# HGRN scores in eight steps with the next pair's preparation between them, and the sums of h taken from kept transposes, one a slot

## The chip, the cores and the metric

The kernel runs on one core of a Trainium2 chip. The metric is the device time of one execution in microseconds. The core has a matrix engine (TensorE, PE in the profile, with its weight loads as PEld), VectorE (DVE), ScalarE (ACT), GpSimd (POOL) and SyncE (SP), which issues DMAs. Each engine works through its own instructions in order; where one needs another's result, it waits on a semaphore.

## The reference

One block of an encoder over 256 positions of width 2048, all in float32:

```
u   = rms_norm(x)                 # over 2048
z   = u @ w_in                    # hq hf hi hg (1024 each), aq ak av (1024 each), gates (4096)
y_a = HGRN2 recurrence of 8 heads on hq hf hi, norm per head, times silu(hg)
y_b = chunked attention of 16 heads on aq ak av, relative bias
h   = x + (sig(gate_a) * (y_a @ w_branch_a) + sig(gate_b) * (y_b @ w_branch_b)) @ w_out
out = rms_norm(h + relu(rms_norm(h) @ w_up)**2 @ w_down)      # w_up 2048x8192, w_down 8192x2048
```

The recurrence is S_t = diag(g_t) S_(t-1) + k_t v_t^T, o_t = S_t^T q_t with g = lb + (1 - lb) * sigmoid(f), k = 1 - g, q = silu(z) / sqrt(128). Written as scores, position t attends to s <= t with q_t * k_s * exp(b_t - b_s), where b is the running sum of log g (started anew every 64 positions, with the decays of whole chunks multiplied in).

## The kernel before, in words

**Products.** Every weight is split into a high part `wh` (ScalarE's cast, line 89) and a remainder `wl` (VectorE's subtraction, line 90), each piece 128x1024, and a product is made of three matmuls, high x high, high x low, low x high (lines 143 to 145 for row blocks, 184 to 188 for transposed ones). So each 128x1024 piece of weights costs a DMA on SP, a cast and a subtraction, and both stand in the queues of ScalarE and VectorE among all else that these do. The casts and subtractions are given priority over the code around them, so the scheduler may set them ahead of it.

**The HGRN stage.** The heads come in pairs, four pairs u = 0 to 3. `fq(u)` makes f and z of a pair (for pairs 2 and 3 by two products, hf and hq) and prepares them: `hf_pair` (lines 310 to 326) scales f, takes the sigmoid, makes kk = 1 - f and clamps f (lines 319, 320), takes the logarithm on ScalarE and the running sum b by a scan on VectorE (line 324); `hq_pair` (lines 328 to 339) makes q from z (line 335) with two copies of odd columns times f (line 338).

`hgrn_scores` makes a pair's scores at several distances. The diagonal (line 372) multiplies kk by q on PE; VectorE writes it into `sd` by a product with the identity (line 373) and a predicated copy (line 374). For each level B = 2, 8, 32, `factors` makes exp(b_end - b) (`el`, lines 383, 384), exp(b - b_start) (`er`, 388, 389 or 393 to 397) and the ratios `rr` (390, 391), the differences on VectorE, the exponentials on ScalarE, and from them `kl` (399) and `qr` (403 to 405); `level` multiplies them on PE (line 416) and copies the result into `sd` under masks (line 423). `factors128` and `level128` (line 448) do the same across the two halves of 128 positions. The five steps of a pair are: diagonal and factors 2; level 2 and factors 8; level 8 and factors 32; level 32 and factors128; level128.

`hgrn_out` makes outputs from scores and values: per head pair and half, `po` on PE (lines 476, 477), its squares on ScalarE (481), their sum (482), `ms` (95), the power on GpSimd (96) and `o` (487), the last two times two; `finish` transposes o (494) and splits it.

These steps are spread by hand over the matmuls of other products: `later` puts steps in the list `behind`, each with a number, `tick` is called once or twice for each 128 rows of a weight, and when a step's number has been counted down it is issued there. All `ps` and `po` tiles share two PSUM buffers (tag `sm`). The order before: pairs 0 and 1 are both prepared at once, then pair 0's scores with a first gap of 20 and gaps of 8, queued ahead of hi (values, `v_chunk(0)`), pair 1's with gaps of 8, then hg, then hf and hq of pair 2, then `group(0)` queues the outputs of the first two pairs, pair 2's scores with gaps of 6, hf and hq of pair 3, values, pair 3's scores, hg, `group(1)`, and the first two products of the attention stage.

**The units.** From the gates on, 512x512 blocks of products go by a scheme of seven block products instead of eight, `Unit` and `run` (lines 725 to 915). It needs sums of blocks of the left matrix: `combos` (lines 632 to 660) adds each block's high and low part into a fresh token buffer (line 640), subtracts and adds these in place (651, 655 to 657) and splits the four results, `S5`, `S4`, `S2`, `S7`. Where `blocks` is given, it takes those instead of line 640's sums; the units of the MLP do so. A unit has some eleven slots, at which `step` issues one entry of its list of steps, if the slot's number is at least the entry's third member, or else the unit's `start`. `plain` issues at once all leading entries whose first member is at most the quarter of the left matrix that it needs.

Unit `wo0` and unit `wo2` make h = x + m @ w_out in four column blocks. During `wo2`, the steps `h_blocks(0)` transpose the blocks 0 and 1 of h (`tp_h`, line 106, two PSUM buffers), scale them by the norm's weights (`hw`, line 981), split them into `act_h`, take the sums of squares on ScalarE (line 983), and make the four sums `S_h` for the next unit, `up00`. In `up00`, `h_blocks(2)` do the same for blocks 2 and 3, and `factor` makes the norm's factors.

Of the kernel before, what the change touches and what calls it, by code (L numbers as in the profile page):

```python
# [18 lines left out]
NM = T // P  # L19
# [31 lines left out]
def tile_hybrid_block(  # L51
# [6 lines left out]
    x, out = x[0], out[0]  # L58
# [100 lines left out]
    def later(*steps):  # L159
        behind.extend([n, f] for n, f in steps)  # L160
# [45 lines left out]
    steps = [1, 1] + [2] * (KD // 2 - 1)  # L206
# [103 lines left out]
    def hf_pair(u, f):  # L310

        nc.vector.tensor_tensor(f, f, bc(rstd_t, 1, 2), op=ALU.mult)
        nc.scalar.activation(f, f, AF.Sigmoid)
        for h in range(2):
            hh = 2 * u + h
            nc.vector.tensor_scalar(f[:, h, :], f[:, h, :], omlb[:, hh:hh + 1], lb[:, hh:hh + 1],
                                    op0=ALU.mult, op1=ALU.add)
        kk = h2(f"kk{u}")
        nc.vector.tensor_scalar(kk, f, -1.0, 1.0, op0=ALU.mult, op1=ALU.add)
        nc.vector.tensor_scalar(f, f, LN_MIN, None, op0=ALU.max)  # L320
        lg = h2(f"lg{u}")
        nc.scalar.activation(lg, f, AF.Ln)
        b = h2(f"b{u}")
        nc.vector.tensor_tensor_scan(b.rearrange("p h t -> p (h t)"), reset,
                                     lg.rearrange("p h t -> p (h t)"), 0.0, ALU.mult, ALU.add)
        return f, kk, b

    def hq_pair(u, z, g):

        nc.vector.tensor_tensor(z, z, bc(rstd_t, 1, 2), op=ALU.mult)  # L330
        s = h2(f"sq{u}")
        nc.scalar.activation(s, z, AF.Sigmoid)
        q = hp.tile([P, 2, NM, 192], F32, name=f"q{u}", tag="q", bufs=2)
        half = lambda a: a.rearrange("p h (m t) -> p h m t", t=P)
        nc.vector.scalar_tensor_tensor(q[:, :, :, 0:P], half(z), DK ** -0.5, half(s), op0=ALU.mult, op1=ALU.mult)
        odd = lambda a: a.rearrange("p h m (j u) -> p h m j u", u=2)[:, :, :, :, 1]
        for h in range(2):
            nc.vector.tensor_tensor(q[:, h, :, P:], odd(q[:, :, :, 0:P])[:, h], odd(half(g))[:, h], op=ALU.mult)
        return q

    def v_chunk(g):
        acc = gemm(xT, w_in_n, C_HI + g * NC, KD, f"hi{g}")
        vs = []
        for m in range(NM):
            v = hp.tile([P, NC], F32, name=f"v{g}{m}", tag="tok", bufs=7)
            nc.scalar.activation(v, acc[:, m, :], AF.Copy, scale=rstd[:, m:m + 1])
            vs.append(v)
        return vs

    def hg_chunk(g):  # L350
        acc = gemm(xT, w_in_n, C_HG + g * NC, KD, f"hg{g}")
        gws = []
        for m in range(NM):
            s = hp.tile([P, NC], F32, name=f"gw{g}{m}", tag="tok", bufs=7)
            nc.scalar.activation(s, acc[:, m, :], AF.Sigmoid, scale=rstd[:, m:m + 1])
            nc.vector.scalar_tensor_tensor(s, acc[:, m, :], rstd[:, m:m + 1], s, op0=ALU.mult, op1=ALU.mult)
            s3 = s.rearrange("p (h d) -> p h d", d=DK)
            nc.vector.tensor_tensor(s3, s3, bc(hgw, 1, NH), op=ALU.mult)
            gws.append(s)
        return gws  # L360

    def hgrn_scores(n, kk, b, q):

        sd = hp.tile([P, 2, NM, P], F32, name=f"sd{n}", tag="sd", bufs=2)
        so = hp.tile([P, 2, P], F32, name=f"so{n}", tag="so", bufs=2)
        held = {}
# [85 lines left out]
        f = [lambda i=i, B=B: factors(i, B) for i, B in enumerate(LEVELS)]  # L452
        l = [lambda i=i, B=B: level(i, B) for i, B in enumerate(LEVELS)]

        def both(*fs):
            def go():
                for x in fs:
                    x()
            return go

        return (sd, so), [both(diagonal, f[0]), both(l[0], f[1]), both(l[1], f[2]), both(l[2], factors128), level128]

    ya = []

    def hgrn_out(g, h0, sc, vs, gws):
        sd, so = sc
        n = f"{g}{h0}"
        hi, lo = ya[g][:, :, 0, :], ya[g][:, :, 1, :]
        os = []

        def outputs(m):
            po = ps_sm.tile([P, 2, DK], F32, name=f"po{n}{m}", tag="sm")
            for h in range(2):
                c = slice((h0 + h) * DK, (h0 + h + 1) * DK)
                if m:
                    nc.tensor.matmul(po[:, h, :], so[:, h, :], vs[0][:, c], start=True, stop=False)
                nc.tensor.matmul(po[:, h, :], sd[:, h, m, :], vs[m][:, c], start=m == 0, stop=True)
            o = hp.tile([P, 2, DK], F32, name=f"o{n}{m}", tag="o", bufs=4)
            sq = hp.tile([P, 2, DK], F32, name=f"osq{n}{m}", tag="osq", bufs=1)
            s2 = small.tile([P, 2], F32, name=f"os{n}{m}", tag="os")  # L480
            nc.scalar.activation(sq, po, AF.Square)
            nc.vector.tensor_reduce(s2, sq, axis=AX.X, op=ALU.add)
            ro = small.tile([P, 2], F32, name=f"ro{n}{m}", tag="ro")
            rsqrt(ro, s2, DK, 2)
            for h in range(2):
                c = slice((h0 + h) * DK, (h0 + h + 1) * DK)
                nc.vector.scalar_tensor_tensor(o[:, h, :], po[:, h, :], ro[:, h:h + 1], gws[m][:, c],
                                               op0=ALU.mult, op1=ALU.mult)
            os.append(o)

        def finish(m):
            tp = ps_tp.tile([P, 2, P], F32, name=f"tpo{n}{m}", tag="tp")
            for h in range(2):
                nc.tensor.transpose(tp[:, h, :], os[m][:, h, :], ident)
            split(hi[:, h0:h0 + 2, m * P:(m + 1) * P], lo[:, h0:h0 + 2, m * P:(m + 1) * P], tp)

        return [lambda m=m: outputs(m) for m in range(NM)], [lambda m=m: finish(m) for m in range(NM)]

    def fq(u):
        if u == 0:  # L500
            f, z = f0, z0
        elif u == 1:
            f, z = f1, z1
        else:
            f, z = h2(f"f{u}"), h2(f"zq{u}")
            add_parts(f, gemm_t(xT, w_in_t, C_HF + u * T, KD, f"hf{u}"))
            add_parts(z, gemm_t(xT, w_in_t, C_HQ + u * T, KD, f"hq{u}"))
        g, kk, b = hf_pair(u, f)
        return kk, b, hq_pair(u, z, g)


    def scores(n, a, gap, first=None):
        sc, steps = hgrn_scores(n, *a)
        later(*[(gap if i or first is None else first, f) for i, f in enumerate(steps)])
        return sc

    def group(g, s0, s1, vs, gws, gap, gap2):
        o0, f0 = hgrn_out(g, 0, s0, vs, gws)
        o1, f1 = hgrn_out(g, 2, s1, vs, gws)
        later(*[(gap, f) for f in o0 + o1], *[(gap2, f) for f in f0 + f1])  # L520

    ya += [new_act(f"ya{g}") for g in range(2)]
    a0, a1 = fq(0), fq(1)
    s0 = scores(0, a0, 8, 20)
    vs0 = v_chunk(0)
    s1 = scores(1, a1, 8)
    gws0 = hg_chunk(0)
    a2 = fq(2)
    group(0, s0, s1, vs0, gws0, 3, 4)
    s2 = scores(2, a2, 6)  # L530
    a3 = fq(3)
    vs1 = v_chunk(1)
    s3 = scores(3, a3, 6)
    gws1 = hg_chunk(1)
    group(1, s2, s3, vs1, gws1, 2, 3)
    acc_q = [gemm_t(xT, w_in_t, C_AQ + i * T, KD, f"aq0{i}") for i in range(2)]
# [90 lines left out]
    def fours(t):  # L627
        return t.rearrange("p (k t) -> p k t", t=P)
# [340 lines left out]
    hT = []  # L969
    Sh = {}  # L970

    def h_blocks(n0):

        def one(n, m):
            if not m:
                hT.append(new_act(f"h{n}"))
            hi, lo = hT[n][:, :, 0, :], hT[n][:, :, 1, :]
            t = h1[n][m]
            tp = transpose4(t, f"h{n}{m}")
            tmp = fours(token(f"hw_{n}_{m}"))  # L980
            nc.vector.tensor_tensor(tmp, tp, bc(wmlp[:, 4 * n:4 * n + 4], 2, P), op=ALU.mult)
            split(hi[:, :, m * P:(m + 1) * P], lo[:, :, m * P:(m + 1) * P], tmp)
            nc.scalar.activation(token(f"hsq_{n}_{m}"), t, AF.Square, accum_out=ssq2[:, m, n:n + 1])

        def factor():
            ssum2 = small.tile([P, NM], F32, name="ssum2", tag="ssum")
            nc.vector.tensor_reduce(ssum2, ssq2, axis=AX.X, op=ALU.add)
            rsqrt(rstd2, ssum2, D, NM)

        return [(n, lambda n=n, m=m: one(n, m)) for n in (n0, n0 + 1) for m in range(NM)] + [  # L990
            (n0 + 1, f, 7) for f in ([factor] if n0 else combos(hT, "h", sp, Sh))]

    rstd2 = const.tile([P, NM], F32, name="rstd2")

    def h_out(m, n, acc):
        t = token(f"h1_{n}_{m}")
        with tc.high_priority(offset=2000):
# [7 lines left out]
    rstd3 = const.tile([P, NM], F32, name="rstd3")  # L1005
    NQ = 4
    units = [Unit(lambda: mT, lambda: Sm, w_out, n0 * NC, f"wo{n0}", lambda m, n, acc, n0=n0: h_out(m, n0 + n, acc),
                  steps=(lambda: h_blocks(0)) if n0 else (lambda: turned(mT, 3, "m3", ga)), start=3 if n0 else 0) for n0 in (0, 2)]
    fin = {}
    for qd in range(NQ):  # L1010
        last = qd == NQ - 1
# [115 lines left out]
```

## Time and profile before

| | us |
|---|---|
| median of three runs | 1410.29 (1409.94 to 1411.42) |
| the profiled execution | 1411.28 |
| its span in the profile | 1409.5 |
| PE busy (98% of the span) | 1387.3 |
| DVE busy (79%) | 1119.1 |
| ACT busy (64%) | 909.0 |
| POOL busy (10%) | 137.0 |

The granted clock of PE averages 0.997 over the span. The HGRN stage lies between about 10 and 240 us of the profile, the units `wo0` and `wo2` between about 640 and 734, and `up00` follows. A row of instructions has start, duration, engine, line, operation, output <- input, shape and count, and in brackets how long the engine stood idle before it and what released it. `wl_hi` is the remainder of a piece of the weights hi, `act_h` the split transposes of h, `acc_up00c` a PSUM bank of unit up00.

### The profile page before, as it was taken

The numbers are of one execution on the slowest core, as the hardware profiler recorded it, in microseconds if no ns is written. First come the engines' busy times: TensorE is split into PE (matmuls) and PEld (weight loads), VectorE is DVE, ScalarE is ACT, GpSimd is POOL, SyncE is SP. The second block draws the span as 40 slices with busy tenths as digits, with TensorE's granted clock in tenths as the row PEclk, the third lists the DMA queues.
The fourth block names the chain that finished last, engine by engine and source line by source line (L and its number), as shares of the span: only waits on it lengthen the run. The fifth ranks groups of instructions, "written<-read, shape, count | busy, mean of one in ns | idle before, by whom it ended". The sixth has DMA issues, their size and how long they took to land.

```text
span 1409.5 us, 18582 instructions
## 1 busy us (share of the span) xinstructions
PE 1387.3 (98%) x6562; PEld 1149.8 (82%) x6562; DVE 1119.1 (79%) x1410; ACT 909.0 (64%) x1170; POOL 137.0 (10%) x220
## 2 busy tenths in 40 slices
PE   9999999999999999999999999999999999999997
PEld 7878888878787888888778888888888888888885
DVE  7897987675657875687999878789777897878885
ACT  6755745464556665445767876677666876668764
POOL 2000001010000000001210001100111001110200
PEclk9999999999999999999999999999999999999999
DMA  9644445665568987558898898998899888998883
GB/s 336 219 156 156 144 157 162 191 172 167 177 224 262 259 236 257 188 176 254 245 292 263 242 277 225 288 279 249 258 290 292 249 229 252 286 298 261 259 247 118
DMA packets 122925, 327.42 MB, mean 232 GB/s; under 512 B 10944, under 2 KB 11712, under 8 KB 122448
## 3 DMA queue, kind: packets, MB, share of 16 engines
q1 hardware_dynamic: 103264, 264.80, 54.8%
q0 software_dynamic: 18416, 59.84, 21.4%
q10 hardware_dynamic: 1152, 1.60, 0.3%
q8 instruction: 51, 0.84, 0.2%
q14 instruction: 42, 0.34, 0.1%
HBM read 271.67 MB, written 10.49 MB: 200 GB/s over the span
## 4 chain that ended last, share of the span: by engine, by line
PE 93%; DVE 3%; ACT 2%; issue 1%; DMA 0%; POOL 0%; SPq 0%; POOLq 0%; DVEq 0%; ACTq 0%
PE acc_ak L185 2%; PE acc_hq L185 2%; PE acc_aq L185 2%; PE acc_hf L185 2%; PE ps L416 1%; PE tp_u L106 1%; PE acc_ga L144 1%; PE acc_hg L144 1%; PE acc_hg L145 1%; PE acc_hg L143 1%; PE acc_ga L145 1%; PE acc_bb L143 1%; PE acc_ga L143 1%; PE acc_ba L143 1%; PE acc_av L145 1%; PE acc_ba L145 1%
## 5 line engine op out<-in xcount | busy, mean ns | idle before, releaser
L185 PE MATMUL acc_aq<-act_x,wh_aq 128*128 128x512 f32 x128 | 46.6, 401 | 0.0
L185 PE MATMUL acc_hf<-act_x,wh_hf 128*128 128x512 f32 x128 | 45.9, 396 | 0.0
L185 PE MATMUL acc_hq<-act_x,wh_hq 128*128 128x512 f32 x128 | 45.9, 396 | 0.0
L185 PE MATMUL acc_ak<-act_x,wh_ak 128*128 128x512 f32 x128 | 45.2, 398 | 0.0
L90 DVE TENSOR_TENSOR wl_ga<-raw_ga,wh_ga 128x1024 fp32r<-128x1024 f32 x16 | 19.6, 1225 | 19.6 <-ACT wh_ga L89 19.4
L184 PE MATMUL acc_aq<-act_x,wl_aq 128*128 128x256 f32 x120 | 34.9, 291 | 0.0
L184 PE MATMUL acc_hf<-act_x,wl_hf 128*128 128x256 f32 x120 | 34.4, 287 | 0.0
L184 PE MATMUL acc_hq<-act_x,wl_hq 128*128 128x256 f32 x120 | 34.3, 286 | 0.0
L90 DVE TENSOR_TENSOR wl_av<-raw_av,wh_av 128x1024 fp32r<-128x1024 f32 x16 | 19.6, 1224 | 18.1 <-ACT wh_av L89 18.1
L184 PE MATMUL acc_ak<-act_x,wl_ak 128*128 128x256 f32 x120 | 33.8, 281 | 0.0
L89 ACT CAST wh_hg<-raw_hg 128x1024 fp32r<-128x1024 f32 x16 | 16.8, 1050 | 24.2 <-PE acc_hg L145 13.9
L89 ACT CAST wh_bb<-raw_bb 128x1024 fp32r<-128x1024 f32 x16 | 16.9, 1054 | 23.3 <-PE acc_ba L145 17.7
L90 DVE TENSOR_TENSOR wl_bb<-raw_bb,wh_bb 128x1024 fp32r<-128x1024 f32 x16 | 19.6, 1222 | 14.8 <-ACT wh_bb L89 14.8
L89 ACT CAST wh_av<-raw_av 128x1024 fp32r<-128x1024 f32 x16 | 16.8, 1052 | 22.0 <-PE acc_av L145 12.4
L90 DVE TENSOR_TENSOR wl_aq<-raw_aq,wh_aq 128x1024 fp32r<-128x1024 f32 x16 | 19.6, 1223 | 14.2 <-ACT wh_aq L89 14.1
L89 ACT CAST wh_ba<-raw_ba 128x1024 fp32r<-128x1024 f32 x16 | 16.8, 1053 | 20.7 <-PE acc_bb L145 13.8
L89 ACT CAST wh_aq<-raw_aq 128x1024 fp32r<-128x1024 f32 x16 | 16.8, 1048 | 20.0 <-PE acc_hg L145 9.5
L90 DVE TENSOR_TENSOR wl_ba<-raw_ba,wh_ba 128x1024 fp32r<-128x1024 f32 x16 | 19.6, 1223 | 12.4 <-ACT wh_ba L89 12.4
L185 PEld LDWEIGHTS acc_ak<-act_x,wh_ak 128*128 128x128 f32 x128 | 24.0, 188 | 5.6
L185 PEld LDWEIGHTS acc_aq<-act_x,wh_aq 128*128 128x128 f32 x128 | 24.1, 189 | 5.4 <-issue 0.7
L185 PEld LDWEIGHTS acc_hf<-act_x,wh_hf 128*128 128x128 f32 x128 | 24.1, 188 | 5.3 <-DVE f L193 0.3
L185 PEld LDWEIGHTS acc_hq<-act_x,wh_hq 128*128 128x128 f32 x128 | 24.1, 188 | 5.1
(1808 smaller groups left out, 5250.3 us busy)
## 6 DMA issues: line engine op xcount, KB each, us to landing
raw_hi<-in_w_in_n_dram SPq DMA_DIRECT2D x16, 512.0 KB, 4.2
raw_hg<-in_w_in_n_dram SPq DMA_DIRECT2D x16, 512.0 KB, 3.8
raw_aq<-in_w_in_t_dram SPq DMA_DIRECT2D x16, 512.0 KB, 4.0
raw_ak<-in_w_in_t_dram SPq DMA_DIRECT2D x16, 512.0 KB, 3.9
raw_av<-in_w_in_n_dram SPq DMA_DIRECT2D x16, 512.0 KB, 4.4
raw_ga<-in_w_in_t_dram SPq DMA_DIRECT2D x16, 512.0 KB, 4.2
raw_ba<-in_w_branch_a_dram SPq DMA_DIRECT2D x16, 512.0 KB, 4.4
raw_bb<-in_w_branch_b_dram SPq DMA_DIRECT2D x16, 512.0 KB, 4.5
```

The source lines that it names most:

```text
L89: (copy or nc.scalar.copy)(hi, src)
L90: nc.vector.tensor_tensor(lo, src, hi.bitcast(F32), op=ALU.subtract)
L106: nc.tensor.transpose(tp[:, j, :], src[:, j * P:(j + 1) * P], ident)
L143: nc.tensor.matmul(acc, hi, wh, start=first, stop=False, skip_group_check=True)
L144: nc.tensor.matmul(acc, hi, wl, start=False, stop=False, skip_group_check=True)
L145: nc.tensor.matmul(acc, lo, wh, start=False, stop=last, skip_group_check=True)
L184: nc.tensor.matmul(acc[:, cb, 0:T], wl[:, c], r[:, 0, :], start=False, stop=False)
L185: nc.tensor.matmul(acc[:, cb, :], wh[:, c], r.rearrange("p u t -> p (u t)"), start=kt == 0, stop=kt == nkt - 1)
L416: nc.tensor.matmul(ps[:, m, :], klf[:, a * P:(a + 1) * P], qrf[:, a * 192:(a + 1) * 192], start=True, stop=True)
```

## The change

1. `fq` no longer prepares a pair; it returns two steps, `decay` (`hf_pair`) and `query` (`hq_pair`), and a dict that they fill. Pairs 0 and 2 run both at once; pair 1's two are put between pair 0's scores, pair 3's are queued with gaps of 3.
2. A pair's scores are eight steps instead of five: diagonal and factors 2; factors 8; level 2; factors 32; level 8; factors128; level 32; level128. They, and the outputs, are built when they are issued. The gaps are 12, then 5 for pair 0, 4 for the others; `group(0)` is queued ahead of hf and hq of pair 2 with gaps 4 and 3 instead of 3 and 4.
3. `combos` for h is given `hw` as blocks, so that line 640's four additions for h are left out, and works in place on these.
4. The steps `h_blocks(0)` have 99 as first member, so `plain` doesn't issue them; `wo2` begins them at slot 2 instead of 3, and the four sums, and `factor`, may come from slot 6 on instead of 7.

No matmul is added or removed.

```diff
-        return (sd, so), [both(diagonal, f[0]), both(l[0], f[1]), both(l[1], f[2]), both(l[2], factors128), level128]
+        def first():
+            diagonal()
+            f[0]()
+
+        return (sd, so), [first, f[1], l[0], f[2], l[1], factors128, l[2], level128]
...
-        g, kk, b = hf_pair(u, f)
-        return kk, b, hq_pair(u, z, g)
+        made = {}
+
+        def decay():
+            made["g"], made["kk"], made["b"] = hf_pair(u, f)
+
+        def query():
+            made["q"] = hq_pair(u, z, made["g"])
+
+        return made, decay, query
...
+        todo = [(gap if i or first is None else first, lambda i=i: one(i)) for i in range(8)]
+        for at, f in between:
+            todo.insert(at, (gap, f))
+        later(*todo)
...
     a0, a1 = fq(0), fq(1)
-    s0 = scores(0, a0, 8, 20)
+    a0[1]()
+    a0[2]()
+    s0 = scores(0, a0[0], 5, 12, ((5, a1[1]), (8, a1[2])))
     vs0 = v_chunk(0)
-    s1 = scores(1, a1, 8)
+    s1 = scores(1, a1[0], 4)
     gws0 = hg_chunk(0)
+    group(0, s0, s1, vs0, gws0, 4, 3)
     a2 = fq(2)
-    group(0, s0, s1, vs0, gws0, 3, 4)
-    s2 = scores(2, a2, 6)
+    a2[1]()
+    a2[2]()
+    s2 = scores(2, a2[0], 4)
     a3 = fq(3)
+    later((3, a3[1]), (3, a3[2]))
     vs1 = v_chunk(1)
-    s3 = scores(3, a3, 6)
+    s3 = scores(3, a3[0], 4)
     gws1 = hg_chunk(1)
     group(1, s2, s3, vs1, gws1, 2, 3)
...
             tmp = fours(token(f"hw_{n}_{m}"))
+            hw[m, n] = tmp
...
-        return [(n, lambda n=n, m=m: one(n, m)) for n in (n0, n0 + 1) for m in range(NM)] + [
-            (n0 + 1, f, 7) for f in ([factor] if n0 else combos(hT, "h", sp, Sh))]
+        return [(n if n0 else 99, lambda n=n, m=m: one(n, m)) for n in (n0, n0 + 1) for m in range(NM)] + [
+            (99, f, 6) for f in ([factor] if n0 else combos(hT, "h", sp, Sh, hw))]
...
-                  steps=(lambda: h_blocks(0)) if n0 else (lambda: turned(mT, 3, "m3", ga)), start=3 if n0 else 0) for n0 in (0, 2)]
+                  steps=(lambda: h_blocks(0)) if n0 else (lambda: turned(mT, 3, "m3", ga)), start=2 if n0 else 0) for n0 in (0, 2)]
```

More of the change, by code (lines that the diff above doesn't have):

```diff
@@ L360, in hg_chunk, with hgrn_scores @@
         return gws
-    def hgrn_scores(n, kk, b, q):
+    def hgrn_scores(n, made):
+        kk, b, q = made["kk"], made["b"], made["q"]
         sd = hp.tile([P, 2, NM, P], F32, name=f"sd{n}", tag="sd", bufs=2)
@@ L453, in hgrn_scores @@
         l = [lambda i=i, B=B: level(i, B) for i, B in enumerate(LEVELS)]
[L455 to L459, printed above, removed]
-        return (sd, so), [both(diagonal, f[0]), both(l[0], f[1]), both(l[1], f[2]), both(l[2], factors128), level128]
+        def first():
+            diagonal()
+            f[0]()
+        return (sd, so), [first, f[1], l[0], f[2], l[1], factors128, l[2], level128]
     ya = []
@@ L507, in fq, with scores, one, outputs @@
             add_parts(z, gemm_t(xT, w_in_t, C_HQ + u * T, KD, f"hq{u}"))
-        g, kk, b = hf_pair(u, f)
-        return kk, b, hq_pair(u, z, g)
-    def scores(n, a, gap, first=None):
-        sc, steps = hgrn_scores(n, *a)
-        later(*[(gap if i or first is None else first, f) for i, f in enumerate(steps)])
+        made = {}
[4 more added lines that the diff above has]
+        return made, decay, query
+    def scores(n, made, gap, first=None, between=()):
+        sc = []
+        steps = []
+        def one(i):
+            if not i:
+                out, fs = hgrn_scores(n, made)
+                sc.extend(out)
+                steps.extend(fs)
+            steps[i]()
+        todo = [(gap if i or first is None else first, lambda i=i: one(i)) for i in range(8)]
+        for at, f in between:
+            todo.insert(at, (gap, f))
+        later(*todo)
         return sc
     def group(g, s0, s1, vs, gws, gap, gap2):
-        o0, f0 = hgrn_out(g, 0, s0, vs, gws)
-        o1, f1 = hgrn_out(g, 2, s1, vs, gws)
-        later(*[(gap, f) for f in o0 + o1], *[(gap2, f) for f in f0 + f1])
+        parts = {}
+        def outputs(h0, sc, m):
+            if not m:
+                parts[h0] = hgrn_out(g, h0, sc, vs, gws)
+            parts[h0][0][m]()
+        later(*[(gap, lambda h0=h0, sc=sc, m=m: outputs(h0, sc, m)) for h0, sc in ((0, s0), (2, s1)) for m in range(NM)],
+              *[(gap2, lambda h0=h0, m=m: parts[h0][1][m]()) for h0 in (0, 2) for m in range(NM)])
     ya += [new_act(f"ya{g}") for g in range(2)]
     a0, a1 = fq(0), fq(1)
-    s0 = scores(0, a0, 8, 20)
+    a0[1]()
+    a0[2]()
+    s0 = scores(0, a0[0], 5, 12, ((5, a1[1]), (8, a1[2])))
     vs0 = v_chunk(0)
-    s1 = scores(1, a1, 8)
+    s1 = scores(1, a1[0], 4)
     gws0 = hg_chunk(0)
+    group(0, s0, s1, vs0, gws0, 4, 3)
     a2 = fq(2)
-    group(0, s0, s1, vs0, gws0, 3, 4)
-    s2 = scores(2, a2, 6)
+    a2[1]()
+    a2[2]()
+    s2 = scores(2, a2[0], 4)
     a3 = fq(3)
+    later((3, a3[1]), (3, a3[2]))
     vs1 = v_chunk(1)
-    s3 = scores(3, a3, 6)
+    s3 = scores(3, a3[0], 4)
     gws1 = hg_chunk(1)
@@ L970, in tile_hybrid_block @@
     Sh = {}
+    hw = {}
     def h_blocks(n0):
```

## The prediction

> **What bounds the kernel now.** I read the page first, then the list of what TensorE waited for, then windows of two microseconds around each wait, then the queues of VectorE and ScalarE ahead of it. From the page: busy time per engine, and the shares of the chain that ended last.
>
> ```profile
> PE 1387.3 (98%) x6562; PEld 1149.8 (82%) x6562; DVE 1119.1 (79%) x1410; ACT 909.0 (64%) x1170; POOL 137.0 (10%) x220
> PE 93%; DVE 3%; ACT 2%; issue 1%; DMA 0%; POOL 0%; SPq 0%; POOLq 0%; DVEq 0%; ACTq 0%
> ```
>
> TensorE (PE) is busy for 1387.3 of 1409.5 us, and the diff adds or removes no matmul. So the change can only win back some of the 22.2 us in which PE stands still, plus time in which its clock is low. The list of PE's waits (line of the waiting matmul, line of what released it; total, count, longest) shows which of these the diff can reach:
>
> ```profile
> PE ps L416 <- DVE qr L405: 2.2, 1, 2.2
> PE acc_wo2c L143 <- ACT u_wo L756: 2.1, 1, 2.1
> PE po L477 <- DVE o L487: 1.1, 1, 1.1
> PE tp_h L106 <- DVE hw L981: 0.8, 1, 0.8
> PE ps L416 <- DVE sd L374: 0.7, 1, 0.7
> PE po L476 <- DVE ms L95: 0.3, 1, 0.3
> ```
>
> That is 7.2 us, four waits in the HGRN scores and outputs, two where h is transposed. The other waits lie in the start, in unit ga2 and in unit wo0, which the diff leaves alone. The clock adds to the first. Windows (busy PE with instructions, PEld, DVE, ACT, POOL, then the granted clock, the DMA share, GB/s):
>
> ```profile
> 72.00:74.00 2.00, 0.55 (x3) 0.13 (x1) 2.00 (x5) 2.00 (x6) 0.00 (x0) 1.00 0.30 123
> 74.00:76.00 2.00, 1.29 (x7) 1.32 (x8) 2.00 (x5) 1.35 (x2) 0.00 (x0) 0.91 0.29 68
> 76.00:78.00 2.00, 2.00 (x7) 1.71 (x6) 2.00 (x8) 0.00 (x0) 0.00 (x0) 0.50 0.69 223
> 78.00:80.00 2.00, 2.00 (x8) 1.54 (x8) 1.08 (x3) 0.73 (x1) 0.00 (x0) 0.73 0.59 231
> 710.00:720.00 10.00, 8.23 (x36) 6.84 (x37) 9.91 (x12) 8.23 (x11) 0.00 (x0) 1.00 0.92 336
> ```
>
> Behind the first wait PE ran below full clock until 80 us: 2 x (0.09 + 0.50 + 0.27) = 1.7 us lost. The equally long wait near 710 was followed by no such loss. So the diff's reach is 7.2 + 1.7 = 8.9 us, 0.6% of the time.
>
> **Part 1: the scores of pair 0.** The queues ahead of the first wait (start, duration, engine, line):
>
> ```profile
> 60.11 0.42 DVE L319 TENSOR_SCALAR kk<-f 128x512 f32<-128x512 f32 x1
> 60.91 0.68 DVE L335 SCALAR_TENSOR_TENSOR q<-zq,sq 128x512 f32<-128x512 f32 x1
> 61.85 1.22 DVE L90 TENSOR_TENSOR wl_hi<-raw_hi,wh_hi 128x1024 fp32r<-128x1024 f32 x1
> 63.39 0.39 DVE L390 TENSOR_TENSOR rr<-b 128x128 f32<-128x128 f32 x1
> 66.17 1.21 DVE L324 TENSOR_TENSOR_SCAN b<-reset,lg 128x512 f32<-128x512 f32 x1
> 68.55 1.23 DVE L90 TENSOR_TENSOR wl_hi<-raw_hi,wh_hi 128x1024 fp32r<-128x1024 f32 x1 [1.18 <-ACT wh_hi L89]
> 70.50 0.69 DVE L335 SCALAR_TENSOR_TENSOR q<-zq,sq 128x512 f32<-128x512 f32 x1
> 71.34 0.52 DVE L338 TENSOR_TENSOR q<-q,f 128x128 f32<-128x128 f32 x2
> 73.14 1.22 DVE L90 TENSOR_TENSOR wl_hg<-raw_hg,wh_hg 128x1024 fp32r<-128x1024 f32 x1
> 74.28 0.29 DVE L405 TENSOR_TENSOR qr<-qr,rr 128x128 f32<-128x128 f32 x1
> 65.64 1.46 PE L372 MATMUL ps<-q,kk 128*128 128x192 f32 x8
> 74.71 1.67 PE L416 MATMUL ps<-qr,kl 128*128 128x192 f32 x7 [2.16 <-DVE qr L405]
> 79.23 0.24 PE acc_hi L143
> 81.74 0.23 PE acc_hi L145
> ```
>
> The rows at 60.11, 66.17, 70.50 and 71.34 are pair 1's preparation, standing in the queue among pair 0's factors. In the changed order the scan, q and the odd columns of pair 1, and the piece of wl_hg, all come behind pair 0's last qr. From start to next start the 128x1024 subtraction takes 1.14 (73.14 to 74.28), q about 0.6, the two L338 0.4. So 1.2 (scan) + 0.6 + 0.4 + 1.1 leave, and with them the 1.18 for which DVE stood before 68.55 while ScalarE was at pair 1's functions: 4.5 in all. qr is ready near 74.6 - 4.5 = 70.1.
>
> Where does PE stand by then? It had reached this level at 74.71 - 2.16 = 72.5. In the changed order it stands 12 matmuls earlier; at 0.23 each (the last two rows, from the chain, are eleven such matmuls apart: 0.228 each) that is 2.7, so 69.8. But the diagonal is also earlier, by 20 matmuls: 65.64 - 4.5 = 61.1. There q is not ready. kk of pair 1 is out of the way, which brings q's start to 60.6; then come q, rr and one head of L338 (half of 0.52), 0.6 + 0.3 + 0.25, so about 61.8: a new wait of 0.7. The second head's L338 stands behind a wl_hi (1.14) and ends near 63.1, when PE has just done the first head's pieces (half of 1.46) and three matmuls (0.7): 0.2 more. So PE loses 0.9 at the diagonal, comes to the first level at 70.7, and finds qr ready with 0.6 to spare. Old wait and low clock go: -3.9; new wait: +0.9 (bounds 0 and 2.2, the wait there was).
>
> Pair 1's scan, q and odd columns aren't free of cost for DVE; they now lie under hi and hg, behind pair 0's levels, which come 38 to 56 matmuls apart (8.6 to 12.7 us) instead of 26. Pair 1's diagonal comes 34 matmuls later than before, its first level 36. That is the cover; nothing is late next there by more than I can see. The diff leaves the order of what SP and GpSimd issue as it was, here and in the parts below, so no DMA and no `pow` is moved past another.
>
> **Part 2: the scores of pairs 2 and 3, and the outputs.** The 0.7 wait (pair 2's first level, behind the diagonal's predicated copies) goes: the spacing between diagonal and first level grows from 20 to 26 matmuls, 6 x 0.228 = 1.4, more than 0.7. Pairs 2 and 3 have 26 matmuls between steps instead of 20: no new wait, bound by the 0.7 now paid. Rows of the output chain of group 0:
>
> ```profile
> 142.53 0.41 DVE L482 TENSOR_REDUCE os<-osq 128x2 f32<-128x256 f32 x1
> 143.26 0.16 DVE L95 TENSOR_SCALAR ms<-os 128x2 f32<-128x2 f32 x1
> 144.26 0.61 DVE L487 SCALAR_TENSOR_TENSOR o<-po,ro,gw 128x128 f32<-128x128 f32 x2 [0.42 <-POOL ro L96]
> 233.45 0.69 POOL L96 TENSOR_TENSOR ro<-ms,mhalf 128x2 f32<-128x2 f32 x1 [2.65 <-DVE ms L95]
> 237.96 0.28 PE L184 MATMUL acc_aq<-act_x,wl_aq 128*128 128x256 f32 x1
> 238.31 0.28 PE L184 MATMUL acc_aq<-act_x,wl_aq 128*128 128x256 f32 x1
> ```
>
> The third po has two PSUM buffers to share, so it waits for the first one's o. The distance of the two is 39 matmuls where it was 41, and the order puts a 128x1024 subtraction in front of the reduce. I leave the 1.1 where it is (bounds -1.1 and +1.1, one subtraction later). In group 1 the third po stands 21 matmuls behind the first where there were 40; the chain 0.41 + 0.16 + 0.69 + 0.61 = 1.9 fits into 21 x 0.175 = 3.7 (the last two rows are two matmuls apart) if nothing stands in front of it. I keep the 0.3 (bounds -0.3 and +1.9).
>
> **Part 3: the h blocks in unit wo2.** DVE, ScalarE and PE there and in the next unit:
>
> ```profile
> 690.00:744.00 54.00, 51.13 (x237) 41.35 (x237) 53.49 (x62) 36.74 (x50) 9.29 (x14) 1.00 0.95 289
> 706.55 1.89 DVE L640 TENSOR_TENSOR a_h<-act_h 128x512 f32<-128x512 f32 x3
> 709.67 0.62 ACT L89 CAST S_h<-a_h 128x512 fp32r<-128x512 f32 x1 [3.82 <-DVE a_h L651]
> 711.14 0.58 ACT L756 COPY u_wo<-acc_wo2c 128x512 f32<-128x512 f32 x1
> 743.05 0.68 DVE L90 TENSOR_TENSOR act_h<-hw,act_h 128x512 fp32r<-128x512 f32 x1
> 743.65 1.21 DVE L90 TENSOR_TENSOR wl_up00p21B<-raw_up00B,wh_up00p21B 128x1024 fp32r<-128x1024 f32 x1
> 743.94 0.39 PE L145 MATMUL acc_up00c<-wh_up00r,act_h 128*128 128x512 f32 x1
> ```
>
> All four blocks of h and all four sums come at the first plain product, so ScalarE's cast of the first sum stands 3.82 waiting for DVE, and a weight cast and the copy u_wo stand behind it. One step a slot takes the sums out of there: u_wo needs only PE. The 2.1 goes, and the 0.8 of the transposes with it (four in a row have two PSUM buffers). Four additions go from DVE, 4 x 0.6 = 2.4. What takes the wait's place: DVE is busy 53.49 of 54 us until 744, so PE cannot run far ahead of it. The low part of h's third block ends at 743.73 and PE uses it at 743.94. In the changed order both subtractions for up00p21B stand before it, 1.1 more. DVE gets there 2.4 + 0.3 of idle time - 1.1 = 1.6 earlier, PE wants it 2.9 - 0.2 = 2.7 earlier: a new wait of 1.1 in up00. So -2.9 + 1.1 = -1.8 (bounds -2.9, all of it; and 0, if DVE gives PE none of its time). The kept transposes hold their token buffers longer, but the summed copies that took four others are gone: 0.
>
> **The sum.** -3.9 + 0.9 - 0.7 - 1.8 = -5.5 us against the profiled execution, which took 1411.28 with its span of 1409.5. The median is 1410.29, 0.99 lower; so 1410.3 - 5.5 = 1404.8. A measurement of this kernel can tell about 0.2%, 2.8 us.
>
> [...] The row at 76 shows half clock behind a wait of 2.2; the row at 710 none behind one of 2.1. [...]
>
> **The rivals.** (a) The half clock at 74 to 80 isn't the wait's: the 1.7 stays, 1406.5. For it speaks the wait at 710 without loss; against it that 74 to 80 lies right behind one of the two longest waits. (b) No new waits: neither q at the diagonal nor h's low part is late: -3.9 - 0.7 - 2.9 = -7.5, 1402.8, with the two po waits gone too 1401.4. Against it DVE's 53.49 of 54. (c) The change moves the wait instead of removing it: qr has only 0.6 to spare; if one more 128x1024 subtraction and ScalarE's casts come ahead, the level is late again by up to 2.2 and the clock falls again. Then 0.9 - 0.7 - 1.8 = -1.6: 1408.7, no change to be told. (d) Slower: the outputs' chains lose their cover. Eight po products share two buffers, the later two of each group of four wait for a chain of reduce, ms, POOL and o; in group 1 their distance is halved and in group 0 the reduce is behind a subtraction. A chain laid bare costs 1.9, and behind each of two subtractions 1.1 more: 4.1 x 4 = 16.4, less the 1.4 paid now, +15.0 - 5.5 = +9.5: 1419.8. It turns slower beyond 0.2% from 5.5 + 2.8 = 8.3 us of waiting on, when more than half of this comes. Against it: half of the distance still covers a bare chain.
>
> **How the numbers follow.** My forecast with its own range 1402.5 to 1407 has 0.48; (a) 0.10; (b) 0.14; (c) 0.14; (d) and whatever else adds more than it takes 0.14, of which 0.12 beyond +0.2%. Faster by over 0.2% (under 1407.5): forecast, (a), (b) and a little of (c), 0.75; within 0.2%: 0.13; slower: 0.12. The range from 1400.8 (a little under all 8.9 won) to 1410 (the upper end of (c)) leaves out some 0.16.
>
> **What would show it.** Right: no wait of ps on qr near 70 and full clock until 100 us; a wait of ps of the diagonal on q near 61 of 0.5 to 1; u_wo gone from PE's waits; one on act_h (L90) near 740 of about 1. Wrong: the wait on qr again, of 1 or more; po waits over 2 us together; h's sums late for unit up00, a wait of acc_up00c on S_h near 725.

## The result, and the profile after

| | before | after |
|---|---|---|
| median of 20 runs, us | 1410.43 (1408.80 to 1413.68) | 1408.54 (1406.51 to 1410.70) |
| profiled execution, us | 1411.28 | 1406.51 |
| its span | 1409.5 | 1404.8 |
| PE busy | 1387.3 | 1386.3 |

The ratio of after to before is 0.9985 (95% interval 0.9978 to 0.9992): 2.1 us less, where 5.5 were forecast. The profiled execution of the changed kernel is its fastest of the twenty, 2.0 under its median, and that of before is 0.85 over its own; so the two profiled executions differ by 4.8 us, and 2.9 of that is not in the medians. The traces tell where waits went; how much a part is worth is read from the runs.

The page of the changed kernel (busy times; shares of the chain):

```profile
PE 1386.3 (99%) x6562; PEld 1148.6 (82%) x6562; DVE 1118.1 (80%) x1406; ACT 909.6 (65%) x1170; POOL 137.3 (10%) x220
PE 93%; DVE 2%; DMA 2%; ACT 1%; issue 1%; POOL 0%; POOLq 0%; SPq 0%; ACTq 0%; DVEq 0%
```

DMA, 0% of before's chain, is in the chain now. Its list of PE's waits:

```profile
PE acc_up00c L145 <- DVE S_h L90: 1.6, 1, 1.6
PE acc_up00c L143 <- ACT wh_up00r L89: 1.2, 1, 1.2
PE po L476 <- DVE o L486: 1.1, 1, 1.1
...
PE ps L373 <- DVE q L338: 0.5, 1, 0.5
...
PE acc_wo2c L144 <- DVE wl_wo2r L90: 0.4, 1, 0.4
PE po L475 <- DVE o L486: 0.3, 1, 0.3
```

All four waits that the prediction took away are gone (qr, u_wo, tp_h, sd); the two on po are where they were, 1.1 and 0.3. New are 0.5 at the diagonal, and in wo2 and up00 three that add to 3.2 (and a fourth of 0.2). The windows of two and ten microseconds:

```profile
74.00:76.00 2.00, 2.00 (x10) 1.66 (x9) 1.86 (x4) 1.99 (x3) 0.00 (x0) 1.00 0.04 14
76.00:78.00 2.00, 2.00 (x10) 1.68 (x9) 1.86 (x3) 1.98 (x4) 0.00 (x0) 1.00 0.69 258
700.00:710.00 10.00, 10.00 (x45) 8.27 (x45) 6.29 (x9) 4.33 (x7) 0.00 (x0) 1.00 1.02 385
720.00:730.00 10.00, 8.46 (x38) 5.86 (x36) 10.00 (x11) 5.36 (x6) 2.79 (x4) 1.00 1.01 302
730.00:740.00 10.00, 8.10 (x35) 6.24 (x36) 9.87 (x12) 7.25 (x12) 0.05 (x1) 1.00 1.01 280
```

The clock is full (1.00) in all of them, where before had 0.91 and 0.50 at 74 and 76. But from 700 to 710 VectorE is busy for 6.29 of 10 us, a stretch in which it had no time to give (9.93 of 10 in before), and 20 us later PE loses 1.5 and 1.9. The rows around it, ScalarE, VectorE and twice PE:

```profile
705.80 1.05 ACT L89 CAST wh_wo2r<-rawp_wo2r 128x1024 fp32r<-128x1024 f32 x1 [4.65 <-DMA rawp_wo2r<-in_w_out_dram]
706.88 1.23 DVE L90 TENSOR_TENSOR wl_wo2r<-rawp_wo2r,wh_wo2r 128x1024 fp32r<-128x1024 f32 x1 [3.68 <-ACT wh_wo2r L89]
730.72 0.50 PE L145 MATMUL acc_up00c<-wh_up00p12C,S_h 128*128 128x512 f32 x1 [1.60 <-DVE S_h L90]
738.99 0.50 PE L143 MATMUL acc_up00c<-wh_up00r,act_h 128*128 128x512 f32 x1 [1.18 <-ACT wh_up00r L89]
```

ScalarE stood 4.65 for a piece of the weights that had not landed, VectorE 3.68 behind ScalarE. The piece itself was hardly slower than before: it was issued at 695.01 and landed 10.7 us later, where in before it was issued at 703.06 and took 9.8. But in before ScalarE came to it only 0.7 after it had landed. The start of each unit's first matmul, after less before: hi -0.6, hg -3.8, ak -5.4, wo2 -5.6, up00 -9.8, up02 -4.8, end -4.7. (The 0.6 at hi lies in the start, which the diff leaves alone.) Up to ak the change wins 4.9; wo2 wins 4.2 more, and up00 gives back 5.0. From wo2's first matmul to up02's, PE stands still for 3.4 us in both kernels: in before all of it ahead of up00's first matmul, in the changed kernel all of it behind.

### The profile page after: what moved, and what is told of

Read it like the earlier page. It is cut to its first block, busy times and chain, and to the rows that moved or that the text cites. A ratio compares the mean times of both kernels' runs of the same rounds, so it can differ in the third digit from the quotient of the medians.

```text
span 1404.8 us, 18581 instructions
## 1 busy us (share of the span) xinstructions
PE 1386.3 (99%) x6562; PEld 1148.6 (82%) x6562; DVE 1118.1 (80%) x1406; ACT 909.6 (65%) x1170; POOL 137.3 (10%) x220
## 4 chain that ended last, share of the span: by engine, by line
PE 93%; DVE 2%; DMA 2%; ACT 1%; issue 1%; POOL 0%; POOLq 0%; SPq 0%; ACTq 0%; DVEq 0%
PE acc_ak L185 2%; PE acc_aq L185 2%; PE acc_hq L185 2%; DMA raw_hf<-in_w_in_t_dram 1%; PE acc_hf L185 1%; PE tp_u L106 1%; PE acc_ga L144 1%; PE acc_ga L145 1%; PE acc_bb L143 1%; PE acc_bb L145 1%; PE acc_hg L145 1%; PE acc_hg L144 1%; PE acc_ba L145 1%; PE acc_av L143 1%; PE acc_ba L143 1%; PE acc_hg L143 1%
## 5 line engine op out<-in xcount | busy, mean ns | idle before, releaser
L89 ACT CAST wh_ga<-raw_ga 128x1024 fp32r<-128x1024 f32 x16 | 16.8, 1051 | 17.6 <-PE acc_ga L145 9.2
```

The source lines that it names most:

```text
L89: (copy or nc.scalar.copy)(hi, src)
```

## The experiments

Each ratio is to runs of before made beside that kernel's. "e1" is the HGRN part alone, and the later ones are read against it and against the whole change (-2.1).

| kernel | ratio to before (95%) | us | VectorE busy, 690 to 740 |
|---|---|---|---|
| before | | | 49.49 |
| the whole change | 0.9985 (0.9978 to 0.9992) | -2.1 | 45.56 |
| e1 HGRN part alone | 0.9972 (0.9963 to 0.9980) | -3.9 | 49.52 |
| e2 h blocks alone | 1.0020 (1.0011 to 1.0029) | +2.8 | |
| e3 kept transposes alone | 1.0005 (0.9996 to 1.0014) | +0.7 | |
| e4 one step a slot alone | 1.0027 (1.0019 to 1.0036) | +3.8 | |
| e5 whole change, four loads less | 0.9972 (0.9961 to 0.9983) | -3.9 | 48.66 |
| e6 e1, four loads less | 0.9969 (0.9958 to 0.9981) | -4.4 | 48.02 |
| e7 whole change, sums at slot 6 | 0.9985 (0.9976 to 0.9994) | -2.1 | 44.95 |
| e8 e1, kept transposes, sums at slot 6 | 0.9966 (0.9953 to 0.9978) | -4.8 | 46.48 |
| e9 e1, preparation up front | 0.9987 (0.9978 to 0.9995) | -1.8 | |
| e10 before, preparation moved | 0.9977 (0.9967 to 0.9987) | -3.2 | |
| e11 e1, four stores more | 0.9973 (0.9963 to 0.9982) | -3.8 | 49.51 |
| e12 whole change, four stores more | 1.0004 (0.9994 to 1.0013) | +0.6 | 44.85 |

The microseconds are 1410 times the ratio's distance from 1. The last column, from one trace each, is given only where wo2 runs at nearly the same time as in e1 or before.

### The parts by themselves: e1 to e4

e1 is the changed code above the h blocks with before's code from there on; e2 the reverse. e3 and e4 are before with:

```diff
 # e3
-            (n0 + 1, f, 7) for f in ([factor] if n0 else combos(hT, "h", sp, Sh))]
+            (n0 + 1, f, 7) for f in ([factor] if n0 else combos(hT, "h", sp, Sh, hw))]
 # e4
-        return [(n, lambda n=n, m=m: one(n, m)) ...
-            (n0 + 1, f, 7) for f in ([factor] if n0 else combos(hT, "h", sp, Sh))]
+        return [(n if n0 else 99, lambda n=n, m=m: one(n, m)) ...
+            (99, f, 6) for f in ([factor] if n0 else combos(hT, "h", sp, Sh))]
...
-  start=3 if n0 else 0) for n0 in (0, 2)]
+  start=2 if n0 else 0) for n0 in (0, 2)]
```

> The change of the HGRN stage alone (eight steps, pair 1's and pair 3's preparation between them, gaps); the h blocks are those of before. The prediction's own steps: -3.9 + 0.9 - 0.7 = -3.7 us against before (ratio 0.9974). A theory from the changed kernel's trace, that the HGRN stage gave about -4.9 there and the h stage took back some 0.8: -4 to -5 us here, so this kernel is faster than the whole change. A theory that the profiled pair flatters the change and the HGRN part wins less in most executions: about -2 us. In the profile, by all of them: no wait of ps on qr near 70, a new wait of ps on q near 61 of 0.5 to 1, the waits of u_wo (2.1) and tp_h (0.8) still there.

> The change of the h blocks alone (kept transposes as blocks, one step a slot); the HGRN stage is that of before. The prediction's step: -1.8 us (ratio 0.9987), with the u_wo wait gone and about 1.1 on h's low part in up00. The rival from the changed kernel's trace: the last weight pieces of wo2 come late because the loads of x and the stores of h run beside them, and up00 loses again what wo2 won: 0 to +1 us, with a wait of ScalarE or VectorE of 3 to 5 us on rawp_wo2r or its cast, and waits of up00 on S_h and wh_up00r of 1 to 2 us each.

> Only the kept transposes as blocks: the four additions of line 640 for h are gone, the order of the steps is that of before. If VectorE's time is what binds (the prediction's step): the u_wo wait shrinks by the three additions that stood ahead of it, from 2.1 to about 0.3, and -1.5 to -2.4 us. If what is won in wo2 is lost to late pieces: 0 to -0.5 us.

> Only the order: one h block a slot, one sum a slot from slot 6, with the four additions kept. The prediction's step: the u_wo wait goes, but the additions' 2.4 us stay with VectorE, so most comes back in up00: -0.5 us at best. The rival: up00 loses more than wo2 wins, +1 to +2 us.

The HGRN part wins 3.9, as the prediction's steps for it say (3.7). The h blocks lose 2.8, where 1.8 was to be won, and it is the order, one step a slot, that loses (e4); the four additions less are worth nothing that can be told (e3). From e3's list of PE's waits:

```profile
PE tp_h L106 <- DVE hw L984: 1.1, 2, 0.9
...
PE acc_up00c L143 <- ACT wh_up00r L89: 0.7, 1, 0.7
```

There the wait on u_wo is gone, where the step left 0.3 of it; the 0.7 is new, and the 1.1 was 0.8 in before. From e2 and then from e4, what VectorE waited for between 680 and 745 us:

```profile
DVE wl_wo2r L90 <- ACT wh_wo2r L89: 4.6, 3, 4.0
```

```profile
DVE wl_wo2r L90 <- ACT wh_wo2r L89: 4.8, 3, 3.9
```

Before and e1 have no such wait, and e3 has 1.4. In e4, PE stands for a remainder that VectorE makes late, longer than for anything in before; VectorE is then behind with its work (busy 10.00 of the 10 us from 720 to 730):

```profile
PE acc_wo2c L144 <- DVE wl_wo2r L90: 3.1, 1, 3.1
```

Part of what e2 and e4 lose is clock behind their waits: 1.7 us in e2's trace and 3.4 in e4's (windows in the last two sections).

So the rival of late pieces stood against a rival of order: that the sums' work is only queued in the wrong place.

### Late pieces or wrong order: e5 to e8

e5 and e6 leave out the loads of x for half of h; e7 and e8 change the steps:

```diff
 # e5 (whole change) and e6 (e1)
+        if n < 2:
             with tc.high_priority(offset=2000):
                 nc.gpsimd.dma_start(t, x[...])
             evict(t, acc)
+        else:
+            with tc.high_priority(offset=2000):
+                nc.vector.tensor_tensor(t..., acc..., bc(ones, 1, NC), op=ALU.add)
 # e7
-            (99, f, 6) for f in ([factor] if n0 else combos(hT, "h", sp, Sh, hw))]
+            (99, f, 6) for f in ([factor] if n0 else [lambda: [g() for g in combos(hT, "h", sp, Sh, hw)]])]
 # e8: e1 with the blocks' own entries as before (n, start 3), and all sums as one entry (99, f, 6), with hw
```

> The changed kernel without the four loads of x (256 KB each) that unit wo2 issues for its two column blocks of h; VectorE adds a constant 1 in their place, so the residual of half the columns is left out. If the late weight pieces (rawp_wo2r, 9.6 us from issue to landing) are late because the DMA engines are full, the pieces land earlier, VectorE's idle stretch of 3.7 us goes, and with it most of the 1.6 + 1.2 of waits in up00: -5 to -6 us against before, 3 to 4 better than the whole change. If the DMA load isn't what matters but the order on VectorE: like the whole change, -2, and the waits in up00 stay.

> The HGRN part alone, with before's h blocks, and without the same four loads of x (a constant is added in their place). The u_wo wait of 2.1 is not a matter of DMA there and stays: -4 us, as the HGRN part alone, to -5 if some other piece of wo2 or up00 had been late too. If this one gains as much by the missing loads as the changed kernel does, the loads say nothing about the h blocks' order.

> The changed kernel with all four sums of h at slot 6 instead of one each at slots 6 to 9. If the loss in up00 is one of order, because VectorE stands 3.7 us behind a late weight piece while the sums' work is queued behind it: the sums fill that stretch, the wait on S_h (1.6) goes and with it 1.5 to 3 us against the whole change, so -3.5 to -5 against before. If it is VectorE's or the DMA's total work: no better than the whole change, -2.

> The HGRN part, h blocks at once as before, kept transposes as blocks, and only the four sums taken to slot 6, behind the copy u_wo. By the prediction's step the u_wo wait of 2.1 goes and 2.4 us leave VectorE: -6 us against before. If what is won in wo2 is lost again in up00 whatever the order: -4, as the HGRN part alone. With as much order trouble as one block a slot: -2.

By the ratios the loads matter to the new order (-3.9 against -2.1) more than to the old one (-4.4 against -3.9, which the intervals don't tell apart). The intervals of e5 and of the whole change overlap a little, so the traces are needed beside them. What ScalarE waited for between 680 and 745 us in e5:

```profile
ACT wh_wo2r L89 <- DMA rawp_wo2r<-in_w_out_dram: 2.6, 2, 1.7
```

With 1 MB of loads less the pieces land 5.6 us after issue in the median instead of 7.1, the waits for them are 2.6 together instead of 4.65, and VectorE has 48.66 of 50 us of work in that stretch instead of 45.56. But e5 isn't better than e1: with the pieces there earlier, VectorE is nearly as full as in before (49.49), and PE still waits in up00 for the sums and the next weights, in e5:

```profile
PE acc_up00c L143 <- ACT wh_up00r L89: 1.2, 1, 1.2
...
PE acc_up00c L145 <- DVE S_h L90: 0.7, 1, 0.7
```

That is 1.9 for the 2.1 of u_wo. This much of the prediction's step holds (a new wait in up00 takes the old one's place), with 1.9 for its 1.1 and at other tiles; 0.7 of it is behind VectorE. e7 gives -2.1 again, but it doesn't test the order: its edit didn't move the sums' work on VectorE. These are e7's rows around the late piece:

```profile
703.88 0.68 DVE L680 TENSOR_TENSOR hw<-hw,hw 128x512 f32<-128x512 f32 x1
708.78 1.23 DVE L90 TENSOR_TENSOR wl_wo2r<-rawp_wo2r,wh_wo2r 128x1024 fp32r<-128x1024 f32 x1 [4.22 <-ACT wh_wo2r L89]
709.93 0.68 DVE L90 TENSOR_TENSOR S_h<-hw,S_h 128x512 fp32r<-128x512 f32 x1
710.53 0.68 DVE L684 TENSOR_TENSOR hw<-hw,hw 128x512 f32<-128x512 f32 x1
```

In the whole change the same four stand in the same order, from 702.52, 706.88, 708.02 and 708.63 on, and in both the other three low parts of the sums come 23 us behind the piece. So the rival of order is open: L684 needs only blocks of h that were made before the piece, yet it stands behind it in VectorE's queue while VectorE waits. A kernel in which it stands ahead was not run.

e8 (-4.8) can't be told from e1. In its trace VectorE stands 3.1 behind pieces, the u_wo wait is gone, and PE waits elsewhere:

```profile
PE tp_h L106 <- DVE hw L1013: 1.5, 2, 0.9
PE acc_up00c L145 <- DVE S_h L90: 1.4, 1, 1.4
...
PE acc_up00c L143 <- ACT wh_up00r L89: 0.7, 1, 0.7
```

### More traffic: e11 and e12

```diff
             t = h1[n][m]
+            if n < 2:
+                nc.gpsimd.dma_start(hd2[n][m], t)
```

> The HGRN part alone, and four more stores of 256 KB each, of h's blocks 0 and 1 to a second place in DRAM, while unit wo2 runs (1 MB more than the kernel needs). If the DMA engines are the limit of that stretch, weight pieces come late here too, with before's order of the h blocks: VectorE idle behind wh_wo2r or wh_up00 and 1 to 3 us lost, so -1 to -3 us against before. If there is room: -4, as without them.

> The whole change with the same four stores more. By the DMA theory the last pieces of wo2 are later still: 1 to 3 us worse than the whole change, so +1 to -1 us against before. If the loss in up00 is not one of DMA: -2, as without them.

With 1 MB more, before's order of the h blocks loses nothing (-3.8 against -3.9); the expectation that it would was wrong. The new order loses 2.7, to +0.6, and there the intervals are apart. The four stores are issued at 675 to 688 us in e11 and at 674 to 686 in e12, so they meet the same stretch. Windows of 50 us, e11 and then e12:

```profile
690.00:740.00 50.00, 47.28 (x216) 38.08 (x215) 49.51 (x57) 33.70 (x47) 7.88 (x12) 1.00 0.97 301
```

```profile
690.00:740.00 50.00, 47.03 (x211) 36.69 (x209) 44.85 (x50) 32.44 (x44) 7.86 (x12) 1.00 0.91 287
```

The DMA engines move less in e12 than in e11 (287 against 301 GB/s), so it isn't their total over the stretch that binds; from 700 to 710, while the piece is under way, they are full in both (shares 1.01 and 1.03). What differs is when the piece is wanted. In e11 VectorE is busy throughout (49.51 of 50 us, no wait behind a piece) and ScalarE waits for none: the piece lands while VectorE works on sums and PE stands at u_wo (2.1), as in before. In the new order (4.2 us further on by up00's start, in the whole change) the piece isn't there; ScalarE waits 5.7 for pieces in e12 and VectorE 5.1 behind it, and VectorE's work for up00 comes late by it.

### What made pair 0's first level late: e9 and e10

```diff
 # e9: e1 with
+    a1[1]()
+    a1[2]()
-    s0 = scores(0, a0[0], 5, 12, ((5, a1[1]), (8, a1[2])))
+    s0 = scores(0, a0[0], 5, 12)
 # e10: before with pair 1's two halves among pair 0's five steps, st0
 # (and, as in the change, pair 1's steps and the outputs built when they are issued)
-    s0 = scores(0, a0, 8, 20)
+    later((20, st0[0]), (8, st0[1]), (8, st0[2]), (4, a1[1]), (4, st0[3]), (4, a1[2]), (4, st0[4]))
```

> The HGRN part with its eight steps, gaps and order, but pair 1's preparation made at once, ahead of pair 0's scores, as before; h blocks of before. If the preparation in VectorE's and ScalarE's queues is what made pair 0's first level late (the prediction's step), the wait of ps on qr is back, and longer than 2.2, since TensorE stands there earlier: 2.5 to 4 with low clock behind it, so 0 to -1.5 us against before. If the finer steps are what helps: -3 to -4, as the HGRN part alone.

> Before with one thing done: pair 1's preparation is put among pair 0's scores (still five steps, gaps of 20 and 8, all else as before). By the prediction's step qr is ready near 70 and TensorE comes at 72.5: no wait and no low clock there, -3.9 us, with the waits of 0.7 (pair 2), 1.1 (po) and those of h still there; no new wait at the diagonal. If the finer steps are needed: 0 to -1.5.

Moving the preparation alone wins 3.2 of the 3.9. One window and one of its waits:

```profile
66.00:82.00 16.00, 16.00 (x78) 13.82 (x77) 15.70 (x38) 12.39 (x17) 0.00 (x0) 1.00 0.51 161
```

```profile
PE ps L416 <- DVE sd L374: 0.7, 1, 0.7
```

PE is busy without a break from 66 to 82 at full clock, and the 0.7 of pair 2 is still there, as expected. e9, with the eight steps and the preparation up front, loses half of e1's gain. The wait on qr is back, though not as I expected (2.5 to 4 at the first level, with low clock): it is 0.3 at the first level, near 71, with full clock (1.00 in every window from 60 to 80), and 1.1 at the next, near 82. The wait of 1.2 on act_ya is new too, and I have no account of it:

```profile
PE ps L417 <- DVE qr L406: 1.4, 2, 1.1
PE tpo L493 <- DVE act_ya L90: 1.2, 1, 1.2
```

So the finer steps help by themselves too. By the ratios the moved preparation does more (-3.2 against e9's -1.8), but the intervals of the two overlap.

## Why the prediction was right or wrong

The measured median, 1408.5, lies in the wide range (1400.8 to 1410) and outside the forecast's own (1402.5 to 1407); within 0.2% of before, which had 0.13. The direction was right, the size 2.6 times too large. The number is that of rival (c), 1408.7, by luck: (c) had the wait on qr come back, and it didn't. Only (c) had drawn the wide range up to 1410. Point by point:

- **The qr wait and the low clock (-3.9): right.** e10 takes the cause away by itself and wins 3.2 (interval 1.8 to 4.7). The rows of the changed kernel that answer to those of before:

```profile
60.00 0.68 DVE L335 SCALAR_TENSOR_TENSOR q<-zq,sq 128x512 f32<-128x512 f32 x1
60.89 0.28 DVE L338 TENSOR_TENSOR q<-q,f 128x128 f32<-128x128 f32 x1
62.23 0.28 DVE L338 TENSOR_TENSOR q<-q,f 128x128 f32<-128x128 f32 x1
68.41 0.29 DVE L406 TENSOR_TENSOR qr<-qr,rr 128x128 f32<-128x128 f32 x1
61.23 0.92 PE L373 MATMUL ps<-q,kk 128*128 128x192 f32 x4 [0.55 <-DVE q L338]
69.93 1.46 PE L417 MATMUL ps<-qr,kl 128*128 128x192 f32 x8
```

  qr is ready at 68.7 and PE comes at 69.9. With the 0.6 by which this trace is ahead at hi, that is 69.3 and 70.5, where 70.1 and 70.7 were forecast: 1.2 to spare instead of 0.6. Rival (c) is out.
- **The new wait at the diagonal (+0.9): right in place and cause, 0.5 in size.** Nothing waited for the second head.
- **Pair 2's 0.7: gone, as said; the po waits: 1.1 and 0.3, as said.** Rival (d), the laid-bare chains, did not happen: half the distance covered them.
- **The low clock (rival a): out.** In each of the four kernels with the 2.2 wait on qr (before, e2, e3, e4) the clock falls to between 0.50 and 0.57 in the window 76 to 78; with the wait gone (the whole change, e1, e10) it is 1.00. The length of a wait didn't settle here whether it cost clock: 2.1 on u_wo cost none in before and e1, and 1.7 in e6 (last section).
- **The h blocks (-1.8): wrong; +2.8 alone (e2), and about +1.8 within the whole change (-2.1 against -3.9).** The step that failed is "what takes the wait's place". It allowed VectorE's time as the only limit, bounded the part at 0 from above, and put the effect on transfers at nothing: no DMA is moved past another, which is so, but the engines now come to a piece sooner. The row that it quoted for 690 to 744 carries a DMA share of 0.95, and the text didn't use it. What the runs showed instead: freed of the waits, the engines come to a piece of wo2's weights before it has landed; VectorE, the engine that had nothing to spare, stands 3.7 behind one; and PE then waits in up00, at the sums (1.6) and the next weights (1.2). That transfers have a part in it is shown by e11 against e12. Whether VectorE need have stood, with work for the sums queued behind the piece, stays open, since e7 left that order as it was. The four additions saved, 2.4 us of VectorE, buy nothing measurable (e3).
- **Rival (b)** named the two places where no new wait would come; both came.

What stays open: why the median of the changed kernel lies 2.0 over its profiled execution, more than before's. One cause can be seen, though not in that kernel: in e2, with the same two waits of up00, of the same length, the clock is low in the windows they lie in, and in the changed kernel's trace it is full (1.00 from 720 to 750). The windows of e2:

```profile
730.00:740.00 10.00, 8.18 (x32) 5.79 (x31) 9.69 (x12) 3.15 (x3) 2.83 (x4) 0.87 1.00 281
740.00:750.00 10.00, 8.82 (x41) 6.93 (x40) 8.50 (x11) 7.71 (x14) 0.00 (x0) 0.96 0.95 294
```

Lost are 10 x (0.13 + 0.04) = 1.7 us. That most executions of the changed kernel lose this, and the profiled one not, would fit, but no trace shows it. Against it speaks e7: its profiled execution is its median one (1408.38), with the same two waits and full clock (1.00 from 710 to 750). Loading x earlier, into buffers of its own, wasn't tried. The HGRN part alone (e1, -3.9) and e8 (-4.8) can't be told apart; e1 is by its ratio 1.8 us better than the whole change, with intervals that overlap a little.

## What to carry to other kernels

Here VectorE was busy 49.49 of 50 us, and the 2.1 taken away at u_wo gave way to 1.6 and 1.2 in the next unit: where an engine is that full, count a removed wait only for what that engine and the transfers of the stretch can follow with, and read the DMA share of the same windows (0.95 here) first. The time of a wait can be the time in which a piece lands: with the work taken out of the queue in front of it, VectorE stood idle for 3.7 us there and PE waited for its sums later. And a step that belongs to the next item, standing in the in-order queues among this one's, is worth moving by itself: here that one move won 3.2 us, where the whole HGRN part won 3.9.

## What the runs showed of the hardware

In these traces the loss of clock came in one size, or twice that. Behind the wait of 2.2 us on qr, the four kernels that have it each lost 1.7 us, for instance e3 and e4 (windows from 74 on, granted clock third from the end):

```profile
74.00:76.00 2.00, 1.52 (x5) 1.55 (x6) 2.00 (x5) 1.11 (x2) 0.00 (x0) 0.57 0.39 98
76.00:78.00 2.00, 2.00 (x8) 1.86 (x7) 1.47 (x5) 0.00 (x0) 0.00 (x0) 0.57 0.60 199
```

```profile
74.00:76.00 2.00, 1.33 (x6) 1.36 (x7) 2.00 (x5) 1.29 (x2) 0.00 (x0) 0.81 0.31 84
76.00:78.00 2.00, 2.00 (x7) 1.81 (x6) 2.00 (x7) 0.00 (x0) 0.00 (x0) 0.50 0.54 205
78.00:80.00 2.00, 2.00 (x9) 1.57 (x8) 1.16 (x4) 0.75 (x1) 0.00 (x0) 0.83 0.62 240
```

2 x (0.43 + 0.43) and 2 x (0.19 + 0.50 + 0.17) are both 1.7. In before, windows of half a microsecond show the low stretch itself: a clock of 0.66 from 75.5 to 76, 0.50 in each from 76 to 79, 0.93 from 79 to 79.5, then 1.00. The wait of 2.1 on u_wo left the clock full (1.00) in before and in e1, and cost as much, 10 x 0.17 = 1.7, in e6, whose wait was as long:

```profile
700.00:710.00 10.00, 7.95 (x29) 6.07 (x28) 9.26 (x13) 5.73 (x8) 0.00 (x0) 0.83 0.82 295
```

Behind e4's wait of 3.1 on wl_wo2r, near 728, twice as much was lost, 10 x (0.14 + 0.20) = 3.4 us:

```profile
720.00:730.00 10.00, 6.88 (x25) 4.84 (x24) 10.00 (x11) 5.45 (x6) 2.89 (x4) 0.86 0.84 179
730.00:740.00 10.00, 9.24 (x39) 7.19 (x38) 8.48 (x12) 3.91 (x7) 1.95 (x3) 0.80 0.94 292
```

So here a wait of about 2 us came with a loss of clock in some cases (2.2 on qr in four traces of four, 2.1 on u_wo in e6) and not in others (2.1 on u_wo in before, e1 and e11), and when it did the price was 1.7. A wait of 1.6 on S_h, together with its neighbours, came with that loss in e2, though not in the whole change and e7 (1.00 from 720 to 750) or in e12 (1.00 over 690 to 740), which have the same two waits. What decides between the two outcomes no run shows.
